# Weight sums made by accumulating loads, one half of x kept on chip, and two more tiles of the pooling gate in the seven-product scheme

## The chip, the cores and the metric

The kernel runs on one core of a Trainium2 chip. The metric is the device time of one execution in microseconds, lower is better; of several executions the median is given. PE is the matrix engine (TensorE), DVE the vector engine, ACT the scalar engine, POOL the GpSimd engine, SP the engine that issues most loads. POOL issues the rest of the transfers, among them all stores of intermediate results.

## The reference

One residual layer over x of 1024 tokens by 1024 channels, float32:

```python
n = rmsnorm(h, norm_mix_pre)
proj = n @ w_in                      # pooling input | q, k, v | xq | three gates of 1024 columns
gates = sigmoid(proj[..., o2:])      # 3 x 1024 channels
y_pool = pool_mixer(p_in, w_pool_mix, pool_scale) @ w_pool_o
y_sb = stick_breaking_attention(q, k, v) @ w_sb_o        # 8 heads, strictly causal
y_x = memory_cross_attention(xq, rmsnorm(mem), w_mem_kv) @ w_x_o
merged = gates[0] * y_pool + gates[1] * y_sb + gates[2] * y_x
h = h + rmsnorm(merged @ w_out, norm_mix_post)
h = h + rmsnorm(swiglu(rmsnorm(h), w_ffn_in) @ w_ffn_out, norm_ffn_post)
```

## The kernel before

Tokens are cut into two halves c = 0, 1 of 512 columns, channels into eight tiles of 128. Each float32 operand is split into a high part (a cast to fp32r on ACT, the first line of `parts` or `split`) and a low part (a subtraction on DVE, the second line), and every product is made as three matmuls (`mm3`: high by high, high by low, low by high).

Projections for a pair of output tiles m, m+1 are a two by two block product, made with seven block products instead of eight (`opening` and `pairs`). Of the weights it needs four quarters b11, b21, b12, b22 (`quarters`, tiles "b", eight slots in all) and three sums of them, t = b12 - b11, then b22 - t, then b21 - t; of the activations it needs A11, A12, A22 and the sums S1 to S4, which are made once before the pairs start and stay in the pools act, a and b1. One block product is 12 matmuls of 512 columns, so a pair is 84. PE's order within a pair is 11, 12 (opening), S1, S2, S4, S3, then the opening of the next pair, then 22. The split weights go through five slots (`wh`, `wl`).

The pairs run for xq, q (two pairs), k (two pairs); then v, in a form of its own with 256 columns; then the pooling gate's tiles 0 to 5 (`PAIRED = 6`, three pairs). Between products, steps of the memory attention and of the pooling mixer are called (`aside`). The remaining gate tiles are made directly, 12 matmuls per unit of (tile, half of the inner sum, half of the tokens): `later` lists 66 such units, and `fill` runs 4 of them before the attention over all tokens ("sticks"), 54 spread over its 32 units by the share of work in each, and 8 after it. Sigmoid, the scan, the mask and the transposes of the sticks run on ACT, DVE, POOL and PE, so the fill units are what PE does meanwhile.

x is loaded once in the beginning (L221, tiles "d") for the pooling input and for the sums of squares, and loaded again in `normed_x` (L256) when the norm is known: half c = 0 around 25 to 33 us into tiles "c" and "d" for A11 and A12, half c = 1 at 55 to 60 us.

Instruction order on each engine is set ahead of the run by a planner that places instructions by priority (roughly the program order) in an estimated timeline; only SP's loads are pinned to the program's order. At run time each engine takes its own list in order and waits on semaphores.

Of the kernel before, what the change touches and what calls it, by code (L numbers as in the profile page):

```python
# [8 lines left out]
F32 = mybir.dt.float32  # L9
F32R = mybir.dt.float32r  # L10
AF = mybir.ActivationFunctionType
ALU = mybir.AluOpType
PSUM = bass.MemoryType.PSUM

P = 128
# [13 lines left out]
LEAD = 8  # L29
HOLD = 3  # L30
EARLY = 3
PAIRED = 6
FILL_FIRST = 4
FILL_LAST = 8
TB = C // P
# [4 lines left out]
def hybrid_block(  # L40
# [47 lines left out]
    def t_act():  # L88
        return act.tile([P, C], F32R, tag="act", name="act")
# [10 lines left out]
    def t_c(dt=F32):  # L100
        return cp.tile([P, C + 16], dt, tag="c", name="c")

    def t_d(dt=F32):
        return dp.tile([P, C + 16], dt, tag="d", name="d")
# [7 lines left out]
    def load(dst, src, queue=nc.sync):  # L112

        if dst.dtype == F32R and queue is not nc.gpsimd:
            dst, src = dst.bitcast(F32), src.bitcast(F32)
        tc.keep_in_program_order(queue.dma_start(dst, src))
# [94 lines left out]
    def pool_step(k):  # L211
        wh, wl = w_units[k]
        for g in range(3):
            for c in range(NC):
                gs = slice(g * P, (g + 1) * P)
                mm3(pp[g][c], wh[:, gs], wl[:, gs], xgh[k][c], xgl[k][c], k == 0, k == KT - 1)

    for k in range(KT):
        for c in range(NC):
            xr = t_d()[:, :C]  # L220
            load(xr, x[k, c])  # L221
            if c == 0:
                w_units[k] = split(w_pool[k], 3 * P)
            nc.scalar.activation(xgh[k][c], xr, AF.Copy, scale=gain(G_PRE, k))
            xgl[k][c] = (t_b1 if k < 4 else t_b2)(F32R)
            nc.vector.scalar_tensor_tensor(
                xgl[k][c], xr, gain(G_PRE, k), xgh[k][c].bitcast(F32), ALU.mult, ALU.subtract
            )
            if k == 0:
                nc.scalar.activation(ssum[c], xr, AF.Square)  # L230
            else:
                sq = t_c()[:, :C]
                nc.scalar.activation(sq, xr, AF.Square)
                nc.vector.tensor_add(ssum[c], ssum[c], sq)
        if k > 3:
            pool_step(k - 4)
# [7 lines left out]

    HK = KT // 2
    A = {n: [None] * HK for n in ("11", "12", "21", "22", "S1", "S2", "S3", "S4")}

# [2 lines left out]
        eng.tensor_sub(lo, src, hi.bitcast(F32))  # L252
        return hi, lo

    def normed_x(k, c, t):
        load(t, x[k, c])  # L256
        nc.vector.scalar_tensor_tensor(t, t, gain(G_PRE, k), rbc[c], ALU.mult, ALU.mult)
        return t

# [16 lines left out]
    units = [split(w_pool_l[half]) for half in range(2)]  # L276
    pc = ps_t()
    rbc = []
    a11 = []
    for c in range(NC):  # L280
        rb = t_r()[:, :C]
        rms_rows(ssum[c], C, pc[:, c * TB : (c + 1) * TB], rb)
        rbc.append(rb)
        pool_step(4 + c)
        if c == 1:
            first_mk = [split(w_mk[0, half]) for half in range(2)]
            first_gate = [t_g(), t_g()]
            for half in range(2):
                load(first_gate[half], w_gate[KT, half])
        else:  # L290
            for q in range(HK):
                a11.append(normed_x(q, 0, t_c()[:, :C]))
                A["11"][q] = parts(a11[q], t_act(), t_act())
    for q in range(4):
        sq = t_c()[:, :C]
        nc.scalar.activation(sq, mr[q], AF.Square)
# [7 lines left out]
    for k in range(6, KT):  # L304
        pool_step(k)
    for q in range(HK):
        u = normed_x(q + HK, 0, t_d()[:, :C])
        A["12"][q] = parts(u, t_act(), t_act())
    raw_d = [
        [dram.tile([P, C], F32, name=f"raw{g}{c}") for c in range(NC)] for g in range(4)  # L310
    ]
# [118 lines left out]
    def quarters(src, m):  # L430

        raw = [[None, None], [None, None]]
        for h, i in ((0, 0), (1, 0), (0, 1), (1, 1)):
            raw[h][i] = t_b2()
            load(raw[h][i], src[m + i, h])
        return raw

    def opening(raw, sink, other=ps_a):
        (b11, b12), (b21, b22) = raw
        X, Y = ps_a(), other()  # L440
        product(X, w_parts(b11), "11", True)
        p1 = copied(X)
        product(Y, w_parts(b21), "12", True)
        nc.vector.tensor_add(p1, Y, p1)
        sink(0, 0, p1)
        return X

    def pairs(jobs, raws=None):

        raws = raws or [jobs[0][0]()]  # L450
        ahead = len(raws)

        opened = [opening(raws[j], jobs[j][1], (ps_a, ps_z)[j]) for j in range(ahead)]
        for j, (_, sink) in enumerate(jobs):
            (b11, b12), (b21, b22) = raws[j]
            if len(raws) == j + 1 < len(jobs):
                raws.append(jobs[j + 1][0]())
            X, Y = opened[j], ps_a()
            t = b11
            nc.vector.tensor_sub(t, b12, t)  # L460
            product(Y, w_parts(t), "S1", True)
            s5 = copied(Y)
            aside()
            nc.vector.tensor_sub(t, b22, t)
            product(X, w_parts(t), "S2")
            s2 = copied(X)
            product(Y, w_parts(b22), "S4")
            nc.vector.tensor_add(s2, Y, s2)
            sink(0, 1, s2)
            aside()  # L470
            nc.vector.tensor_sub(b12, b22, b12)
            product(X, w_parts(b12), "S3")
            nc.vector.tensor_add(s5, X, s5)
            sink(1, 1, s5)
            nc.vector.tensor_sub(b21, b21, t)
            if len(opened) == j + 1 < len(jobs):
                opened.append(opening(raws[j + 1], jobs[j + 1][1]))
            product(X, w_parts(b21), "22")
            sink(1, 0, X)
            aside()  # L480

# [40 lines left out]
    for q in range(HK):  # L522
        room = t_d if q < 3 else t_r
        sums[q], a22[q] = normed_x(q, 1, room()[:, :C]), normed_x(q + HK, 1, room()[:, :C])
        nc.vector.tensor_add(sums[q], sums[q], a22[q])
        A["S1"][q] = parts(sums[q], t_act(), t_act())
    xq_raws = [quarters(w_xq, 0)]
    early(1)
    xq_raws.append(quarters(w_q, 0))
    early(2)  # L530
    for q in range(HK):
        nc.vector.tensor_sub(sums[q], sums[q], a11[q])
        A["S2"][q] = parts(sums[q], t_a(F32R), t_a(F32R))
    for q in range(HK):
        u = t_c()[:, :C]
        nc.vector.tensor_sub(u, A["12"][q][0].bitcast(F32), sums[q])
        nc.vector.tensor_add(u, A["12"][q][1].bitcast(F32), u)
        A["S4"][q] = parts(u, t_a(F32R), t_a(F32R))
    for q in range(HK):
        nc.vector.tensor_sub(sums[q], a22[q], sums[q])  # L540
        A["S3"][q] = parts(sums[q], t_b1(F32R), t_b1(F32R))
    for q in range(HK):
        A["22"][q] = parts(a22[q], t_act(), t_act())
# [221 lines left out]
            split_v(ts[b // 2][:, (b % 2) * W : (b % 2 + 1) * W], 4, t)  # L765
            nc.gpsimd.dma_start(v_d[c * TB + b][i], t)

    def sub2(dst, x_, y_):
        for j in range(2):
            nc.vector.tensor_sub(dst[j], x_[j], y_[j])  # L770

    (b11, b12), (b21, b22) = raw
    X, Y = [ps_a(), ps_a()], [ps_a(), ps_z()]
# [5 lines left out]
        nc.vector.tensor_add(p2[i], X[i], p2[i])  # L779
    to_values(0, 0, p2)  # L780
    aside()
    sub2(b11, b12, b11)
    v_product(Y, two(b11), "S1", True)
    s5 = [copied(t) for t in Y]
    aside()
    sub2(b11, b22, b11)
    v_product(X, two(b11), "S2")
    s2 = [copied(t) for t in X]
    aside()
    v_product(Y, two(b22), "S4")  # L790
    for i in range(2):
        nc.vector.tensor_add(s2[i], Y[i], s2[i])
    to_values(0, 1, s2)
    aside()
    sub2(b12, b22, b12)
    v_product(X, two(b12), "S3")
    for i in range(2):
        nc.vector.tensor_add(s5[i], X[i], s5[i])
    to_values(1, 1, s5)
    aside()  # L800
    sub2(b21, b21, b11)
    v_product(X, two(b21), "22")
    to_values(1, 0, X)

# [596 lines left out]
```

## Time and profile before

| | us |
|---|---|
| median of 3 runs (1493.18 to 1497.05) | 1496.27 |
| the profiled execution's own time | 1493.03 |
| its span in the trace | 1491.3 |
| PE busy | 1446.5 (97%) |
| DVE busy | 1032.1 (69%) |
| ACT busy | 702.0 (47%) |
| POOL busy | 333.6 (22%) |

Read by stages: 0 to 53 us pooling input, to 66 us keys and values of the memory, to 99 us the first direct gate units and the openings of xq and q, to 211 us the pairs of xq, q and k, to 254 us v, to 335 us the three pairs of the pooling gate, to about 630 us the sticks with the fill units, then the merge, the output projection and the feed-forward part. Matmuls overlap, so a PE that is busy throughout a stretch is best measured by the number of matmuls in it.

### The profile page before, as it was taken

What the parts mean: (1) busy time and instruction counts of PE and PEld (TensorE: products, weight loads), DVE (VectorE), ACT (ScalarE), POOL (GpSimd) and SP (SyncE); (2) the same over time, 40 slices, a digit from 0 to 9 for tenths busy, and PEclk for the clock granted to TensorE, in tenths of its full rate; (3) what the DMA queues carried; (4) which work ended last, traced back from release to release, by engine and by line L of the source; (5) the groups of instructions that cost most, each with busy time, mean ns of one, the idle gap of its engine ahead of it and who ended that gap; (6) DMA issues with size and microseconds to landing.
All of it is one profiled execution on the core that took longest, in us unless ns stands there. A gap on an engine that the chain in (4) does not pass through costs nothing.

```text
span 1491.3 us, 21003 instructions
## 1 busy us (share of the span) xinstructions
PE 1446.5 (97%) x6926; PEld 1201.3 (81%) x6926; DVE 1032.1 (69%) x1722; ACT 702.0 (47%) x1399; POOL 333.6 (22%) x612
## 2 busy tenths in 40 slices
PE   9989999889999899999999999999999999999997
PEld 8768889668888788878887777888888887788876
DVE  8797878786876878654515597765566666579476
ACT  8555655444655666521235673233333333444453
POOL 0211121222422432454445310000011111000011
PEclk9989999999999999999999999999999999999999
DMA  8724455565432441585455454444455555664445
GB/s 282 247 74 138 154 180 171 184 211 191 129 103 89 151 126 65 172 265 156 148 163 191 148 183 150 152 128 125 140 195 190 195 191 198 233 191 153 109 129 196
DMA packets 126222, 245.77 MB, mean 165 GB/s; under 512 B 16656, under 2 KB 20256, under 8 KB 126112
## 3 DMA queue, kind: packets, MB, share of 16 engines
q1 hardware_dynamic: 97952, 173.09, 37.3%
q0 software_dynamic: 27584, 70.29, 13.6%
q8 instruction: 54, 0.88, 0.2%
q10 hardware_dynamic: 576, 1.05, 0.2%
q14 instruction: 56, 0.46, 0.1%
HBM read 174.11 MB, written 69.73 MB: 164 GB/s over the span
## 4 chain that ended last, share of the span: by engine, by line
PE 84%; DVE 6%; issue 4%; DMA 3%; ACT 2%; POOL 1%; SPq 0%; POOLq 0%; DVEq 0%; ACTq 0%
PE pa L170 17%; PE pa L172 17%; PE pa L171 17%; PE pz L172 5%; PE pz L171 5%; PE pz L170 5%; PE pt L172 3%; PE pt L170 3%; PE pt L171 3%; PE pt L893 2%; PE pv L908 1%; PE pv L905 1%; PE pv L171 1%; PE pv L170 1%; PE pv L172 1%
## 5 line engine op out<-in xcount | busy, mean ns | idle before, releaser
L170 PE MATMUL pa<-act,wh 128*128 128x512 f32 (+1 forms) x584 | 230.6, 395 | 10.8 <-ACT wh L164 3.5
L172 PE MATMUL pa<-act,wl 128*128 128x512 f32 (+1 forms) x584 | 229.8, 396 | 3.9 <-DVE wl L252 3.8
L171 PE MATMUL pa<-act,wh 128*128 128x512 f32 (+1 forms) x584 | 230.0, 394 | 0.0
L251 ACT CAST wh<-b 128x512 fp32r<-128x512 f32 x152 | 93.5, 621 | 146.4 <-PE pa L171 86.3
L170 PEld LDWEIGHTS pa<-act,wh 128*128 128x128 f32 x584 | 111.3, 191 | 34.8 <-issue 4.1
L172 PEld LDWEIGHTS pa<-act,wl 128*128 128x128 f32 x584 | 111.4, 191 | 27.0 <-DVE wl L252 5.2
L171 PEld LDWEIGHTS pa<-act,wh 128*128 128x128 f32 x584 | 111.1, 190 | 20.9
L252 DVE TENSOR_TENSOR wl<-b,wh 128x512 fp32r<-128x512 f32 x152 | 103.2, 685 | 30.7 <-ACT wh L251 26.0
L164 ACT CAST wh<-ws 128x512 fp32r<-128x512 f32 (+1 forms) x119 | 72.7, 612 | 104.4 <-PE pa L171 34.2
L251 ACT CAST wh<-ws 128x512 fp32r<-128x512 f32 x80 | 49.9, 625 | 106.6 <-DVE ws L1165 42.1
L165 POOL TENSOR_TENSOR wl<-ws,wh 128x512 fp32r<-128x512 f32 x52 | 69.3, 1340 | 72.4 <-ACT wh L164 70.1
L251 ACT CAST d<-b 128x512 fp32r<-128x512 f32 x66 | 40.7, 620 | 90.6 <-PE pt L171 45.8
L252 DVE TENSOR_TENSOR d<-b,d 128x512 fp32r<-128x512 f32 x66 | 45.3, 689 | 51.0 <-ACT d L251 50.9
L165 DVE TENSOR_TENSOR wl<-ws,wh 128x512 fp32r<-128x512 f32 (+1 forms) x67 | 44.7, 672 | 51.7 <-ACT wh L164 31.0
L170 PE MATMUL pa<-a,wh 128*128 128x512 f32 x192 | 75.9, 398 | 2.6 <-ACT wh L251 1.2
L171 PE MATMUL pa<-b,wh 128*128 128x512 f32 x192 | 75.0, 392 | 0.0
L172 PE MATMUL pa<-a,wl 128*128 128x512 f32 x192 | 74.6, 392 | 0.0
L176 DVE TENSOR_TENSOR d<-pt,d 128x512 fp32r<-128x512 f32 (+1 forms) x96 | 60.6, 637 | 16.9 <-ACT d L175 16.1
L1131 POOL DMA_DIRECT2D ff<-c x44 | 23.8, 542 | 214.9 <-DVE c L1186 123.6
L175 ACT CAST d<-pt 128x512 fp32r<-128x512 f32 (+1 forms) x96 | 53.0, 559 | 36.4 <-PE pt L893 25.5
L252 DVE TENSOR_TENSOR wl<-ws,wh 128x512 fp32r<-128x512 f32 x80 | 54.9, 688 | 17.8 <-ACT wh L251 15.4
L181 POOL TENSOR_TENSOR rc<-rv,mhalf 128x1 f32<-128x1 f32 (+2 forms) x15 | 14.5, 969 | 229.8 <-DVE rv L1294 198.3
(422 smaller groups left out, 4026.7 us busy)
## 6 DMA issues: line engine op xcount, KB each, us to landing
b<-in_w_ffn_in_dram SPq DMA_DIRECT2D x88, 256.0 KB, 2.8
d<-gt SPq DMA_DIRECT2D x48, 256.0 KB, 2.8
ws<-in_w_ffn_in_dram SPq DMA_DIRECT2D x44, 256.0 KB, 2.7
ff<-c POOLq DMA_DIRECT2D x44, 256.0 KB, 3.2
b<-ffS SPq DMA_DIRECT2D x44, 256.0 KB, 2.6
ws<-in_w_gate_dram SPq DMA_DIRECT2D x40, 256.0 KB, 3.4
gt<-g POOLq DMA_DIRECT2D x39, 256.0 KB, 2.8
b<-ff SPq DMA_DIRECT2D x33, 256.0 KB, 3.6
```

What stands on the lines that cost most here:

```text
L164: nc.scalar.copy(wh[:, :n], ws[:, :n])
L165: lo.tensor_sub(wl[:, :n], ws[:, :n], wh[:, :n].bitcast(F32))
L170: nc.tensor.matmul(ps, lh, rh, start=first, stop=False, skip_group_check=onto)
L171: nc.tensor.matmul(ps, lh, rl, start=False, stop=False, skip_group_check=onto)
L172: nc.tensor.matmul(ps, ll, rh, start=False, stop=last, skip_group_check=onto)
L175: nc.scalar.copy(hi, ps)
L176: nc.vector.tensor_sub(lo, ps, hi.bitcast(F32))
L251: nc.scalar.copy(hi, src)
L252: eng.tensor_sub(lo, src, hi.bitcast(F32))
L893: nc.tensor.transpose(ptr[:, col + n * P : col + (n + 1) * P], att[i, j // 4][:, (j % 4) * P : (j % 4 + 1) * P], ident,)
L905: nc.tensor.matmul(po[:, :wd], vs, al[:, at : at + wd], start=j2 == t2 and n == 0, stop=False)
L1131: nc.gpsimd.dma_start(ff_d[n][k], t)
```

## The change

Three edits. (1) In `quarters`, `opening` and `pairs` the DVE subtractions that made the weight sums are gone. The signs of S1, S2, S3 and S4 are turned so that each sum is an addition, and the addition is done by a transfer that POOL issues (`onto`): it reads a quarter of the weights again from DRAM and adds it to what lies in the tile. The tile of b11 goes through b11, b11 + b21 ..., each step after the parts of the last were taken. The results of S4 and S3 are now subtracted from (`less`, a three-operand instruction on DVE). For v the sums stay on DVE, with other signs. (2) Half c = 0 of x is loaded into eight tiles of the pool act (32 slots) and stays there; it is scaled in place and read for A11, A12 and the sums S2 and S4, where S4 takes one instruction per tile instead of two. (3) `PAIRED` is 8: the pooling gate's tiles 6 and 7 become a fourth pair, and `later` shrinks from 66 units to 58.

```diff
-PAIRED = 6
+PAIRED = 8
...
+    xs = []
     for k in range(KT):
         for c in range(NC):
-            xr = t_d()[:, :C]
+            if c == 0:
+                xr = act.tile([P, C], F32, tag="act", name="act")
+                xs.append(xr)
+            else:
+                xr = t_d()[:, :C]
             load(xr, x[k, c])
...
-    def normed_x(k, c, t):
-        load(t, x[k, c])
+    def normed_x(k, c, t, kept=False):
+        if not kept:
+            load(t, x[k, c])
...
-                a11.append(normed_x(q, 0, t_c()[:, :C]))
-                A["11"][q] = parts(a11[q], t_act(), t_act())
+                A["11"][q] = parts(normed_x(q, 0, xs[q], True), t_act(), t_act())
...
-        u = normed_x(q + HK, 0, t_d()[:, :C])
-        A["12"][q] = parts(u, t_act(), t_act())
+        A["12"][q] = parts(normed_x(q + HK, 0, xs[q + HK], True), t_act(), t_act())
...
-        return raw
+        onto(raw[0][1], src[m + 1, 1])
+        return raw, src[m : m + 2]
+
+    def onto(t, src):
+        nc.gpsimd.dma_start(t, src, accum_op=ALU.add)
+
+    def less(t, ps):
+        nc.vector.scalar_tensor_tensor(t, ps, -1.0, t, ALU.mult, ALU.subtract)
 
     def opening(raw, sink, other=ps_a):
-        (b11, b12), (b21, b22) = raw
+        ((b11, _), (b21, _)), src = raw
         X, Y = ps_a(), other()
         product(X, w_parts(b11), "11", True)
+        onto(b11, src[1, 0])
         p1 = copied(X)
...
-            (b11, b12), (b21, b22) = raws[j]
+            ((t, t3), (_, b22)), src = raws[j]
...
-            t = b11
-            nc.vector.tensor_sub(t, b12, t)
             product(Y, w_parts(t), "S1", True)
+            onto(t, src[1, 1])
             s5 = copied(Y)
             aside()
-            nc.vector.tensor_sub(t, b22, t)
             product(X, w_parts(t), "S2")
+            onto(t, src[0, 1])
             s2 = copied(X)
             product(Y, w_parts(b22), "S4")
-            nc.vector.tensor_add(s2, Y, s2)
+            less(s2, Y)
             sink(0, 1, s2)
             aside()
-            nc.vector.tensor_sub(b12, b22, b12)
-            product(X, w_parts(b12), "S3")
-            nc.vector.tensor_add(s5, X, s5)
+            product(X, w_parts(t3), "S3")
+            less(s5, X)
             sink(1, 1, s5)
-            nc.vector.tensor_sub(b21, b21, t)
             if len(opened) == j + 1 < len(jobs):
                 opened.append(opening(raws[j + 1], jobs[j + 1][1]))
-            product(X, w_parts(b21), "22")
+            product(X, w_parts(t), "22")
...
-        nc.vector.tensor_add(sums[q], sums[q], a22[q])
+        nc.vector.tensor_sub(sums[q], a22[q], sums[q])
...
-        nc.vector.tensor_sub(sums[q], sums[q], a11[q])
+        nc.vector.scalar_tensor_tensor(
+            sums[q], sums[q], -1.0, xs[q], ALU.mult, ALU.subtract
+        )
...
-        u = t_c()[:, :C]
-        nc.vector.tensor_sub(u, A["12"][q][0].bitcast(F32), sums[q])
-        nc.vector.tensor_add(u, A["12"][q][1].bitcast(F32), u)
+        u = xs[q + HK]
+        nc.vector.scalar_tensor_tensor(u, u, -1.0, sums[q], ALU.mult, ALU.subtract)
...
-        nc.vector.tensor_sub(sums[q], a22[q], sums[q])
+        nc.vector.scalar_tensor_tensor(
+            sums[q], sums[q], -1.0, a22[q], ALU.mult, ALU.subtract
+        )
```

## Rows read from the trace of the kernel before

**Rows 1.** The page's first part: busy us, share of the span, instructions.

```profile
PE 1446.5 (97%) x6926; PEld 1201.3 (81%) x6926; DVE 1032.1 (69%) x1722; ACT 702.0 (47%) x1399; POOL 333.6 (22%) x612
```

**Rows 2.** What PE waited for, 66 to 335 us: total us, times, longest.

```profile
PE pa L170 <- ACT wh L164: 3.5, 1, 3.5
PE pa L170 <- DVE d L359: 3.5, 1, 3.5
PE pa L172 <- DVE wl L252: 2.2, 1, 2.2
```

**Rows 3.** Stretches: length, then busy us (instructions) of PE, PEld, DVE, ACT, POOL; clock; DMA.

```profile
98.40:113.00 14.60, 10.56 (x29) 7.32 (x28) 12.84 (x22) 5.42 (x11) 2.14 (x4) 0.65 0.41 126
281.00:335.00 54.00, 50.02 (x214) 39.39 (x212) 46.72 (x84) 27.35 (x47) 12.10 (x23) 1.00 0.59 186
350.00:630.00 280.00, 273.77 (x1521) 233.67 (x1520) 221.47 (x340) 166.51 (x370) 96.90 (x255) 1.00 0.38 121
370.00:430.00 60.00, 58.06 (x329) 49.63 (x328) 54.41 (x85) 39.12 (x88) 20.87 (x64) 1.00 0.38 117
490.00:510.00 20.00, 16.54 (x82) 12.62 (x83) 18.86 (x27) 14.30 (x32) 13.19 (x20) 1.00 0.43 148
510.00:610.00 100.00, 100.00 (x565) 86.11 (x564) 83.17 (x127) 61.37 (x134) 33.61 (x95) 1.00 0.32 100
1000.00:1050.00 50.00, 50.00 (x222) 41.42 (x221) 26.16 (x40) 19.23 (x33) 2.71 (x5) 1.00 0.44 136
```

**Rows 4.** PE in order of time, 98 to 112 us: start, us, instruction, idle before.

```profile
99.35 0.47 PE L170 MATMUL pa<-act,wh 128*128 128x512 f32 x1 [0.59 <-DVE c L444]
...
102.26 0.79 PE L172 MATMUL pa<-act,wl 128*128 128x512 f32 x1 [2.22 <-DVE wl L252]
...
106.27 0.63 PE L172 MATMUL pa<-act,wl 128*128 128x512 f32 x1
108.13 0.80 PE L170 MATMUL pa<-a,wh 128*128 128x512 f32 x1 [1.24 <-ACT wh L251]
```

**Rows 5.** DVE's groups, 76 to 109 us: busy us, mean ns, idle before.

```profile
L537 DVE TENSOR_TENSOR c<-act,c 128x512 f32<-128x512 f32 x4 | 2.7, 684 | 0.0
L460 DVE TENSOR_TENSOR b<-b,b 128x512 f32<-128x512 f32 x2 | 1.4, 683 | 0.0
L471 DVE TENSOR_TENSOR b<-b,b 128x512 f32<-128x512 f32 x2 | 1.4, 683 | 0.0
```

**Rows 6.** DVE in order of time, 98 to 109.5 us: start, us, instruction.

```profile
100.32 0.68 DVE L471 TENSOR_TENSOR b<-b,b 128x512 f32<-128x512 f32 x1
...
101.53 0.68 DVE L252 TENSOR_TENSOR wl<-b,wh 128x512 fp32r<-128x512 f32 x1
...
106.34 0.68 DVE L464 TENSOR_TENSOR b<-b,b 128x512 f32<-128x512 f32 x1
...
108.14 0.68 DVE L475 TENSOR_TENSOR b<-b,b 128x512 f32<-128x512 f32 x1
108.75 1.28 DVE L252 TENSOR_TENSOR wl<-b,wh 128x512 fp32r<-128x512 f32 x2
```

**Rows 7.** DVE, ACT and PE in order of time, in the first pair of k.

```profile
162.72 0.68 DVE L252 TENSOR_TENSOR wl<-b,wh 128x512 fp32r<-128x512 f32 x1
...
164.42 0.62 ACT L251 CAST wh<-b 128x512 fp32r<-128x512 f32 x1 [0.96 <-DVE b L464]
...
169.22 0.39 PE L170 MATMUL pa<-a,wh 128*128 128x512 f32 x1
```

**Rows 8.** POOL's group of k's stores: busy us, mean ns, idle before.

```profile
L558 POOL DMA_DIRECT2D k<-d x16 | 8.5, 533 | 26.3 <-ACT d L251 22.9 <-DVE d L252 2.6 <-DVE st L592 0.5
```

**Rows 9.** Transfers, 255 to 335 us: issuing queue, count, KB each, median us to landing.

```profile
v<-d POOLq DMA_DIRECT2D x12, 256.0 KB, 4.7
...
gt<-c POOLq DMA_DIRECT2D x9, 256.0 KB, 2.3
```

**Rows 10.** DVE by form: a three-operand instruction with a PSUM source.

```profile
L686 DVE SCALAR_TENSOR_TENSOR d<-pv,g_sb,d 128x512 fp32r<-128x512 f32 x8 | 6.0, 748 | 4.8 <-ACT d L685 4.8
```

More of the change, by code (lines that the diff above doesn't have):

```diff
@@ L278, in hybrid_block @@
     rbc = []
-    a11 = []
     for c in range(NC):
@@ L766, in to_values, with add2 @@
             nc.gpsimd.dma_start(v_d[c * TB + b][i], t)
-    def sub2(dst, x_, y_):
+    def add2(dst, x_):
         for j in range(2):
-            nc.vector.tensor_sub(dst[j], x_[j], y_[j])
+            nc.vector.tensor_add(dst[j], dst[j], x_[j])
     (b11, b12), (b21, b22) = raw
@@ L781, in hybrid_block @@
     aside()
-    sub2(b11, b12, b11)
+    add2(b11, b12)
     v_product(Y, two(b11), "S1", True)
@@ L785, in hybrid_block @@
     aside()
-    sub2(b11, b22, b11)
+    add2(b11, b22)
     v_product(X, two(b11), "S2")
@@ L791, in hybrid_block @@
     for i in range(2):
-        nc.vector.tensor_add(s2[i], Y[i], s2[i])
+        less(s2[i], Y[i])
     to_values(0, 1, s2)
     aside()
-    sub2(b12, b22, b12)
+    add2(b12, b22)
     v_product(X, two(b12), "S3")
     for i in range(2):
-        nc.vector.tensor_add(s5[i], X[i], s5[i])
+        less(s5[i], X[i])
     to_values(1, 1, s5)
     aside()
-    sub2(b21, b21, b11)
+    add2(b21, b11)
     v_product(X, two(b21), "22")
```

## The prediction, made before the changed kernel was run

> **What bounds the kernel now.** I read the page's busy line first: PE works 97% of the span, every other engine 69% or less [rows 1]. So only two things can shorten the run: fewer matmuls, or less of PE's idle time and low clock. Next the windows: in a full stretch PE gets through 222 matmuls of 512 columns in 50 us [rows 3], that is 50 / 222 = 0.225 us each, 2.70 us for a block product of 12 and 18.9 us for a pair of 84. Then the waits of PE over the stages that the change touches: the three longest are a gate weight at 69 us (3.5), v's last evictions at 267 us (3.5) and a low part of weights at 100 us (2.2) [rows 2]. The reader is to see that the edits reach only the third. The timeline of PE shows what it costs: the product S1 of xq begins at 99.35, stops for 2.22 at its third matmul, and S2 of xq begins only at 108.13 [rows 4]. Meanwhile the granted clock falls: it averages 0.65 over 98.4 to 113, against 1.00 in the full stretches, so part of it ran at 1.2 instead of 2.4 GHz [rows 3]. The instructions from 102.26 to 106.27 are 10 and the next 8 begin at a spacing of about 0.43 us, 0.20 more than at full clock.
>
> **Why there.** DVE is the cause: from 76 to 109 us its groups have no idle time before them [rows 5], and it starts one instruction about every 0.60 us (108.14 to 108.75 [rows 6]). It works through the sums of activations, which come first in the program, and through the weights' sums; the low part of S1 of xq is made at 101.53 and that of S2 at 108.75 [rows 6].
>
> **The change part by part.**
>
> *Products.* Tiles 6 and 7 of the pooling gate cost 2 x 2 x 2 units of 12 matmuls, 96; as a pair they cost 84. 12 x 0.225 = 2.7 us less on PE, which is the bound, so it counts in full: -2.7.
>
> *DVE's queue at 76 to 109 us.* Removed: the second instruction of S4 (L537, 4), the weight subtractions L460 and L471 (2 each) [rows 5] and one each of L464 and L475 [rows 6]: 10 x 0.60 = 6.0 us. Added: 12 of the activation sums become three-operand instructions, 748 ns by the nearest row [rows 10] against 684 [rows 5], 12 x 0.06 = 0.7. Ahead of S1's low part stand seven of the ten, so it starts at about 101.5 - 4.2 + 0.6 = 97.9 and PE runs S1 straight on, done near 101.5. S2 of xq was allowed by DVE at 108.75; now near 108.75 - 6.0 + 0.7 = 103.4. But its weights now come by a transfer that can start only when S1's low part is read: 98.6 + D + a cast of 0.62, where D is issue and landing of an accumulating load. PE would start S2 near 103.7 instead of 108.13, 4.4 less, and its first 8 matmuls would run at full clock, 8 x 0.20 = 1.6 less: together -6.0. Bounds: -7.6 if no wait is left at all (0.59 + 2.22 + 1.24 of idle [rows 4] and 18 x 0.20 = 3.6 of clock), and 0 or above if D is long. A gap of 2.2 before S2 remains possible, and the clock fell behind a gap of 2.22 before [rows 4], which would take back some 2 us, so I take -5.0.
>
> *D.* No accumulating load is in the trace. POOL's issue takes 0.53 us [rows 8]; plain transfers of the same 256 KB from POOL's queue land 2.3 us after issue, 4.7 where the queue is full of v's small pieces [rows 9]. An accumulating load also has to read the tile that it adds to. Lower end 0.5 + 2.3 = 2.8, upper end 0.5 + 2 x 4.7 = 9.9; I take 0.5 + 4.0 = 4.5, nearer the row under load. The Trainium skill ("DMA: Bandwidth & Descriptors", Anatomy of one DMA) gives such a POOL-issued transfer about 2 us plus its bytes over 436 GB/s, an estimate of 2.6 us; the median rows here lie on both sides of it. By it S2 of xq would wait for DVE alone, and the sum would change by 0.3 us.
>
> *The other pairs.* Nine pairs carry four accumulating loads each. Where does the chain through t have room? In the first pair of k, S1's low part starts at 162.72 and ends at 163.40; S2's cast is at 164.42 and PE uses it at 169.22 [rows 7]. The room is 169.22 - 163.40 - 0.62 = 5.2 us, and D = 4.5 fits. In the other links (11 to S1, S2 to 22) two or more products of 2.7 us lie between, and the sum in b12's tile is made ahead. So nothing is added at this D; at 9.9, 4.7 us per pair. What goes from DVE is four instructions of 0.68 a pair. In the gate pairs DVE is busy 46.7 of 54.0 us and PE idles 4.0 [rows 3]; taking 2.5 pairs x 2.7 = 6.8 us off DVE should about halve that: -2.0 (bounds 0 and -4). POOL gains 36 issues of 0.53, 19 us over stages of 250 us, on an engine that is 22% busy [rows 1]; it takes its queue in order, though, so a sum may stand behind a store that waits for an eviction, and the store behind a sum whose readers are late. The Trainium skill (the same page, Two DMAs through the same engine are not ordered) has it that a transfer which depends on another must be held at the issuing engine until the first has landed. So POOL waits for the load of b12 before each first sum, with the sink's stores behind it. No row shows such a wait; I price it inside D's bounds.
>
> *The fourth pair.* 84 matmuls are in the products' term; its own idle time by the other gate pairs is 4.0 / 2.5 = 1.6 us, half of it with DVE relieved: +0.8.
>
> *Fewer fill units.* Inside the sticks 54 units become 46, so PE has 8 x 2.70 = 21.6 us less to do in the 280 us that hold nearly all of it; that is the other side of the pair's 18.9. DVE there is busy 221.5 of 280, 79%; after, four splits fewer, (221.5 - 2.7) / (280 - 21.6) = 85%. Where DVE is at 83% (510 to 610) PE idles nowhere; where it is at 91 to 94% (370 to 430 and 490 to 510, 73.3 of 80 us) PE idles 1.94 + 3.46 = 5.4 of 80, or 6.8% [rows 3]. 85% is nearest the first: (84.7 - 83.2) / (91.6 - 83.2) x 6.8% x 258 = 3.0: +3.0; bounds 0 and +11 (the whole step from 79% to 85% on that slope).
>
> *x kept on chip.* Eight loads fewer; they landed before 53 us, where PE runs without a pause, so nothing (bounds 0 and -1). S1's parts now take slots that the memory's parts leave at 66 us; they are needed at 99. The gate weight that PE waits 3.5 us for at 69 us [rows 2] is behind the loads for half c = 1, which stay. Two sums join that burst: up to +2, not counted.
>
> Sum: -2.7 - 5.0 - 2.0 + 0.8 + 3.0 = -5.9 us. Against the profiled execution, 1493.0, that is 1487.1. It lies 3.2 below the median of the runs shown, so I put the same difference on the median: 1496.3 - 5.9 = 1490.4.
>
> **The rivals.**
> *Slow sums (slower than before).* D decides, from about 5.2 us on, where S2 becomes late in each pair. At D = 7.5: 2.3 us in each of 8 pairs = 18, and at xq the whole -5.0 goes. 1490.4 + 18 + 5 = 1513. For it: another stream to read, POOL's order, DMA shares of 0.41 to 0.59 in these stages [rows 3]. Against it: every plain row from this queue is under 5. Chance 0.21.
> *Starved sticks (no change).* PE follows DVE once there are fewer fill units: +11 instead of +3.0, 1498. For it 370 to 430, against it 510 to 610 [rows 3]. Chance 0.15.
> *The queue at 98 us is only exchanged (no change).* S2 of xq waits for its transfer instead of DVE; the -5.0 is gone, 1495. For it: 103.7 and 103.4 stand close, so each us of D counts. Chance 0.14.
> *The change doesn't do what it says:* the planner lays out all engines by estimated times, and may put S4 before S2 or let a late sum block ACT's queue; inside the ranges above.
>
> **How the numbers follow.** The forecast has a chance of 0.50, its own range 1483 to 1493. Within 0.3% (4.5 us) of before, about what runs of this kernel can tell from no change, lie the second and third rival: 0.29. Slower 0.21. Faster 0.50. The range goes from 1481 (no wait left at 98 us, no starved sticks) to 1505, which takes in slow sums up to D of about 6.5.
>
> **What would show it.** Right: S2 of xq starts near 104 instead of 108.1, clock above 0.9 over 98 to 113; accumulating loads landing in 4 us or less; PE's idle share in the sticks under 4%; DVE's busy time about 19 us less (36 instructions of 0.68 gone, 30 longer by 0.06, the new pair 4 more). Wrong: casts of weights that wait for a POOL transfer with PE idle behind them in the pairs of k and the gate; landings above 5 us; idle PE before transposes and values in the sticks above 10 us.

## The result, and the profile after

The changed kernel takes 1509.05 us (median of 4 runs, 1505.63 to 1511.21) against 1494.72 of the kernel before in the same comparison: a ratio of 1.0099, interval 1.0079 to 1.0118. It is slower by 14.3 us, where 5.9 us less had been forecast, and lies 4 us above the upper end of the range.

The section on the change names the first sum wrongly: the tile of b11 goes b11, then b11 + b12, then + b22, then + b21, for src[1, 0] is the quarter b12.

The busy line of the kernel after, beside [rows 1], then its line for the transfers that POOL issues (packets, MB, and the time of these packets as a share of 16 engines' span):

```profile
PE 1451.4 (96%) x6914; PEld 1205.0 (80%) x6914; DVE 1014.1 (67%) x1692; ACT 704.8 (47%) x1405; POOL 361.2 (24%) x648
...
q0 software_dynamic: 32768, 79.73, 17.4%
```

The same line of the kernel before:

```profile
q0 software_dynamic: 27584, 70.29, 13.6%
```

PE has 12 matmuls fewer and DVE is busy 18.0 us less, as the change intends. PE is idle 13 us longer, though (1509.2 - 1451.4 = 57.8 against 1491.3 - 1446.5 = 44.8), and its busy time is 4.9 us longer in spite of the missing matmuls. POOL's queue grew by 9.44 MB, 36 x 256 KB, but its share of the engines by (17.4% x 1509.2 - 13.6% x 1491.3) / 36 = 1.66 us of all 16 engines for each added transfer.

Where it is lost is seen in the windows. Columns as in [rows 3]. The kernel after: the stretch of S2 of xq, one in the gate pairs, the sticks, and all from the first pair to the end of the gate pairs:

```profile
98.40:113.00 14.60, 11.48 (x37) 8.49 (x37) 6.78 (x12) 4.82 (x9) 3.41 (x5) 0.77 0.71 178
281.00:335.00 54.00, 53.71 (x230) 43.82 (x231) 42.34 (x78) 26.83 (x46) 20.06 (x31) 0.98 0.83 216
390.00:655.00 265.00, 252.67 (x1408) 215.22 (x1407) 211.38 (x330) 158.47 (x355) 93.49 (x250) 0.99 0.36 112
...
100.00:365.00 265.00, 241.04 (x1246) 204.32 (x1247) 173.86 (x359) 130.22 (x277) 77.66 (x126) 0.95 0.70 188
```

The kernel before, 100 to 365 us:

```profile
100.00:365.00 265.00, 251.04 (x1313) 212.13 (x1313) 202.19 (x404) 138.25 (x292) 55.71 (x108) 0.97 0.57 177
```

DVE, which stood in front of PE before, does 28 us less there, and PE gets through 67 matmuls fewer (of several sizes, so the count is rough). The DMA engines' share rose from 0.57 to 0.70; in the gate pairs it is 0.83 where it was 0.59 [rows 3]. Marks in PE's timeline of several profiled executions tell the same by stages (the last column is the last matmul into pt that reads weights; the kernel before has three gate pairs, the others four, and a pair is 18.9 us). The execution of the kernel after that was profiled is its slowest, 1511.2 us, so its marks lie some us later than the medians do:

| us | S2 of xq starts | v starts | v ends | last S3 of the gate ends | into pt |
|---|---|---|---|---|---|
| before | 108.1 | 211.1 | 257.6 | 330.0 | 738.6 |
| after | 102.2 | 216.0 | 262.4 | 365.9 | 757.6 |
| after, sums on DVE | 102.9 | 208.6 | 255.5 | 350.8 | 740.1 |
| after, no sums | 93.4 | 199.0 | 246.3 | 338.6 | 730.9 |
| sums on DVE, loads into dead tiles | 104.7 | 214.3 | 261.7 | 362.5 | 753.5 |

So 5.9 us are won up to S2 of xq, 10.8 lost from there to v, nothing in v (which has no such load), and some 12 more in the gate pairs than the pair that was added. Behind 760 us the kernels run alike.

What PE waits for after, 66 to 365 us:

```profile
PE pa L170 <- ACT wh L257: 10.1, 4, 3.9
...
PE pz L603 <- DVE st L605: 2.9, 1, 2.9
```

The second of these can be followed back. All engines of the kernel after in order of time, first pair of k:

```profile
159.76 0.68 DVE L258 TENSOR_TENSOR wl<-b,wh 128x512 fp32r<-128x512 f32 x1
...
161.01 0.89 POOL L445 DMA_DIRECT2D b<-in_w_k_dram  x1 [5.39 <-DVE st L605]
...
164.94 1.66 ACT L257 CAST wh<-b 128x512 fp32r<-128x512 f32 x3 [3.58 <-DMA b<-in_w_k_dram]
165.59 1.29 DVE L258 TENSOR_TENSOR wl<-b,wh 128x512 fp32r<-128x512 f32 x2 [3.75 <-ACT wh L257]
...
166.92 0.76 DVE L605 TENSOR_REDUCE st<-pz 128x1 f32<-128x256 f32 x2
...
167.73 0.58 PE L603 MATMUL pz<-c,r 128*128 128x256 f32 x1 [2.90 <-DVE st L605]
```

S1's low part ends at 160.44, POOL issues the sum (the releaser named is the DVE instruction behind that low part), ACT casts S2 at 164.94: D is 4.5 us, the forecast's value. PE does not run out of S2, but DVE waits 3.75 us in its own queue for that cast, the reduction for the memory attention stands behind it, and PE waits 2.90 us for the reduction. The room of 5.2 us in the forecast had been read up to PE's use of S2 alone.

POOL's groups after, 60 to 365 us (busy us, mean ns of one, idle before), beside [rows 8]:

```profile
L572 POOL DMA_DIRECT2D k<-d x16 | 9.2, 649 | 27.2 <-ACT d L257 22.9 <-DVE d L258 3.7 <-issue 0.6
...
L445 POOL DMA_DIRECT2D b<-in_w_k_dram x8 | 7.1, 934 | 20.0 <-DVE wl L258 8.1 <-DMA b<-in_w_k_dram 6.5 <-DVE st L605 5.4
```

Transfers after, 66 to 355 us (median us to landing):

```profile
k<-d POOLq DMA_DIRECT2D x16, 256.0 KB, 4.1
...
b<-in_w_gate_dram POOLq DMA_DIRECT2D x16, 256.0 KB, 5.7
...
r<-xq SPq DMA_DIRECT2D x16, 128.0 KB, 3.8
b<-in_w_k_dram SPq DMA_DIRECT2D x8, 256.0 KB, 6.6
b<-in_w_k_dram POOLq DMA_DIRECT2D x8, 256.0 KB, 4.2
```

And before, same stretch:

```profile
k<-d POOLq DMA_DIRECT2D x16, 256.0 KB, 3.5
...
r<-xq SPq DMA_DIRECT2D x16, 128.0 KB, 2.9
b<-in_w_k_dram SPq DMA_DIRECT2D x8, 256.0 KB, 5.4
```

An accumulating load's issue keeps POOL 0.93 us, not 0.53, and it lands in 4.2 to 5.7 us. Its neighbours in these rows, from either queue, land later too. The Trainium skill ("DMA: Bandwidth & Descriptors", Issuing engines are not separate DMA queues) says that transfers run on the same 16 engines whichever engine issued them. The rows for k fit that, since SP's loads went from 5.4 to 6.6 us; not every group does (v's stores went from 4.6 to 3.8 us).

### The profile page after: what moved, and what is told of

Its sections match the earlier page's. It is cut to its first block, busy times and chain, and to the rows that moved or that the text cites. A ratio compares the mean times of both kernels' runs of the same rounds, so it can differ in the third digit from the quotient of the medians.

```text
span 1509.2 us, 21025 instructions
## 1 busy us (share of the span) xinstructions
PE 1451.4 (96%) x6914; PEld 1205.0 (80%) x6914; DVE 1014.1 (67%) x1692; ACT 704.8 (47%) x1405; POOL 361.2 (24%) x648
## 3 DMA queue, kind: packets, MB, share of 16 engines
q0 software_dynamic: 32768, 79.73, 17.4%
HBM read 181.45 MB, written 69.73 MB: 166 GB/s over the span
## 4 chain that ended last, share of the span: by engine, by line
PE 74%; issue 8%; DMA 7%; DVE 6%; POOL 3%; ACT 2%; SPq 0%; POOLq 0%; DVEq 0%; ACTq 0%
PE pa L170 14%; PE pa L172 13%; PE pa L171 13%; PE pz L172 5%; PE pz L170 5%; PE pz L171 5%; PE pt L170 3%; PE pt L171 3%; PE pt L172 3%; DMA b<-in_w_gate_dram 2%; PE pt L907 1%; DMA ws<-in_w_gate_dram 1%; PE pv L919 1%; PE pv L922 1%; PE pv L170 1%
## 5 line engine op out<-in xcount | busy, mean ns | idle before, releaser
L170 PE MATMUL pa<-act,wh 128*128 128x512 f32 (+1 forms) x568 | 224.0, 394 | 8.1 <-DVE d L363 2.9
L171 PE MATMUL pa<-act,wh 128*128 128x512 f32 (+1 forms) x568 | 222.5, 392 | 0.0
L172 PE MATMUL pa<-act,wl 128*128 128x512 f32 (+1 forms) x568 | 220.8, 392 | 1.3 <-DVE wl L258 1.2
L257 ACT CAST wh<-b 128x512 fp32r<-128x512 f32 x159 | 96.8, 620 | 158.8 <-PE pa L171 68.8
L258 DVE TENSOR_TENSOR wl<-b,wh 128x512 fp32r<-128x512 f32 x159 | 107.7, 686 | 56.5 <-ACT wh L257 48.0
L170 PEld LDWEIGHTS pa<-act,wh 128*128 128x128 f32 x568 | 107.7, 190 | 32.2 <-ACT wh L257 4.2
L172 PEld LDWEIGHTS pa<-act,wl 128*128 128x128 f32 x568 | 107.5, 189 | 23.4 <-DVE wl L258 2.1
L171 PEld LDWEIGHTS pa<-act,wh 128*128 128x128 f32 x568 | 107.7, 190 | 20.5 <-issue 0.2
L257 ACT CAST wh<-ws 128x512 fp32r<-128x512 f32 x76 | 47.4, 624 | 109.2 <-DVE ws L1179 39.8
L170 PE MATMUL pa<-a,wh 128*128 128x512 f32 x200 | 81.7, 412 | 11.1 <-ACT wh L257 9.3
L257 ACT CAST d<-b 128x512 fp32r<-128x512 f32 x66 | 40.8, 621 | 91.9 <-PE pt L171 47.0
L172 PE MATMUL pa<-a,wl 128*128 128x512 f32 x200 | 79.7, 402 | 0.0
L171 PE MATMUL pa<-a,wh 128*128 128x512 f32 x160 | 65.0, 406 | 0.0
L888 DVE TENSOR_TENSOR_SCAN r<-a,zero 128x512 f32<-128x512 f32 (+1 forms) x64 | 53.5, 843 | 16.1 <-POOL a L876 15.5
```

What stands on the lines that cost most here:

```text
L170: nc.tensor.matmul(ps, lh, rh, start=first, stop=False, skip_group_check=onto)
L171: nc.tensor.matmul(ps, lh, rl, start=False, stop=False, skip_group_check=onto)
L172: nc.tensor.matmul(ps, ll, rh, start=False, stop=last, skip_group_check=onto)
L257: nc.scalar.copy(hi, src)
L888: nc.vector.tensor_tensor_scan(ex[:, lo + 1 : C + 1], rest[:, lo:], zero.broadcast_to([P, C - lo]), start, ALU.mult, ALU.add,)
```

## The experiments

The two theories that last longest stood at first. **A**, the chain: casts of weights wait in ACT's and DVE's in-order queues for an accumulating load, as at 164.94. **C**, the transfers: an accumulating load takes so much of the 16 engines that loads and stores around it come late, whoever waits for it. A third, **B**, came up on the way: POOL's in-order queue, in which a load waits until DVE has made a low part and stores stand behind it. (In the first four expectations B is another rival, that the fourth pair starves the sticks.) Each run is told as its median and its ratio to the kernel before, run beside it, with the 95% interval.

**Parts of the change.** All sums on DVE (e1), six tiles paired (e2), the sum loads alone (e3), x kept alone (e5).

```diff
# e1, on the changed kernel (all four sums alike)
-            onto(t, src[1, 1])
+            nc.vector.tensor_add(t, t, b22)
             product(X, w_parts(t), "S2")
# e2
-PAIRED = 8
+PAIRED = 6
# e3: e2 with x loaded again in normed_x;  e5: e1 with PAIRED = 6
```

e1: 

> The changed kernel with all weight sums back on DVE (additions, new signs), x kept, eight paired tiles. Theory A (a cast of a summed tile waits in ACT's in-order queue for POOL's transfer, and what stands behind it on ACT and DVE is late): the pairs of q and k lose their 10.8 us and the gate pairs some 9 us, so about 1489 us, and no cast waits for a transfer from POOL. Rival B (the fourth pair starves the sticks, the sums are harmless): about 1505. Rival C (DMA traffic and slower stores, not the waits): about 1489 as well; later runs tell A from C.

e2: 

> The changed kernel with six paired tiles of the pooling gate as before, sums by transfers and x kept stay. Theory A: the sums' losses in q and k (10.8 us) and in three gate pairs (about 6 us) stay, the fourth pair's and the sticks' (about 10 us) go: about 1500. Rival B: about 1489, below the kernel before. Rival C: about 1500.

e3: 

> The kernel before with the weight sums made by accumulating loads and nothing else (x loaded twice, six paired tiles, S4 in two instructions). Theory A: slower than before, about 1503 (10.8 in q and k, about 6 in the gate pairs, less up to 6 us gained at 98 us where DVE is full). Rival B: 1489 to 1495. Rival C: about 1503.

e5: 

> The kernel before with x's first half kept and the S4 sums in one instruction, weight sums on DVE, six paired tiles. Theory A and B: four of DVE's instructions fewer ahead of 101 us, so S1 and S2 of xq 2 to 3 us earlier: 1490 to 1493. Rival D (keeping x costs by slots of act): 1495 or more.

Measured: e1 1492.89 us, 0.9991 (0.9979 to 1.0003). e2 1501.72, 1.0053 (1.0036 to 1.0070). e3 1501.24, 1.0055 (1.0034 to 1.0076). e5 1493.58, 0.9997 (0.9986 to 1.0009). Sticks starved by the fourth pair would have left e1 at 1505, so that rival fell. The whole loss goes with the sum loads: they cost 1509.1 - 1492.9 = 16 us with eight tiles paired and 1501.7 - 1493.6 = 8 us with six. Keeping x (with S4 in one instruction) is worth nothing, and the pair of tiles 6 and 7 nothing that can be told apart (e1 against e5). Why the price per pair rises with the fourth pair (8 us for 8 pairs, 16 for 9) was not settled.

**What the sums cost.** No sums (e4): the four accumulations are left out, so the products use other weights. Plain loads in their place (e6): same tiles, same waits, the data replace instead of adding.

```diff
# e4
-            onto(t, src[1, 1])
# e6
-        nc.gpsimd.dma_start(t, src, accum_op=ALU.add)
+        nc.gpsimd.dma_start(t, src)
```

e4: 

> The changed kernel with the four accumulating loads left out and nothing in their place: the products S1, S2, S3 and 22 take the quarter as it was loaded, so the weight sums are missing from the computation. Theory A (casts wait for transfers): back to about 1490, like the sums on DVE (1492.9) and at most 3 us lower, for DVE has slack there. Rival C (traffic): the same, 1488 to 1492.

e6: 

> The changed kernel with plain loads from POOL's queue in place of the accumulating ones, same tiles, same waits, so the tile holds the last quarter instead of the sum. Theory A: any transfer on the chain costs nearly the same, 1502 to 1509, issue 0.5 instead of 0.9 us and landing about a us sooner. Rival E (accumulation itself is what is slow): below 1497.

Measured: e4 1484.39, 0.9919 (0.9897 to 0.9942); e6 1495.32, 0.9999 (0.9983 to 1.0015). Without sums and loads the kernel is 10.5 us faster than the kernel before and 8.5 faster than e1, which differs from e4 by DVE's sums; both theories had expected less. The accumulating loads cost 24.7 us against none, and 13.7 of these go when the same loads only write: e6 lies where rival E, the accumulation itself, had put it, and not where theory A had. The line of POOL's transfers, e6:

```profile
q0 software_dynamic: 30464, 79.73, 15.6%
```

The same bytes at a smaller share of the engines: (15.6% x 1497.2 - 13.6% x 1483.6) / 36 = 0.88 us each (e4's line has 13.6% too), about half of an accumulating load's 1.66.

**The chain or the transfers.** e8 has DVE's sums and issues the four accumulating loads into tiles that nobody reads any more, so no cast waits for one. e9 shortens the chain instead: the sums of S1 and S2 are built ahead in tiles of their own, for two more plain loads and one more accumulating load a pair.

```diff
# e8, on e1
+            onto(b22, src[1, 0])      # behind the last reader of b22
             product(X, w_parts(b12), "S3")
+            onto(b12, src[1, 1])
...
             nc.vector.tensor_add(b21, b21, t)
+            onto(t, src[0, 1])
...
             product(X, w_parts(b21), "22")
+            onto(b21, src[0, 0])
# e9, on the changed kernel
+        u = [t_c()[:, :C], t_c()[:, :C]]
+        for i in range(2):
+            load(u[i], src[m, 0])
+            onto(u[i], src[m + 1, 0])
+        onto(u[1], src[m + 1, 1])
```

e8: 

> Weight sums on DVE (the variant that took 1492.9), and four accumulating loads a pair beside them, each into a tile whose last reader is done, so that no cast waits for one: POOL's issues and the bytes of the changed kernel without its waits. Theory A: 1493 to 1497. Rival C (traffic, slower stores, POOL's time): 1503 to 1509.

e9: 

> The changed kernel with the sums of S1 and S2 built in tiles of their own, straight after the loads (two more loads by SP and one more accumulating load a pair), so that no cast of theirs waits for the readers of the product before; only the sum for 22 follows S2's parts. Theory A: most of the loss goes, 1493 to 1500, though the traffic is higher. Rival C: 1509 or more.

Measured: e8 1509.34, 1.0092 (1.0074 to 1.0109); e9 1513.13, 1.0118 (1.0101 to 1.0135). Theory A fell as the whole cause: with no cast waiting for the data, the loads cost 16.4 us over e1, as much as the changed kernel loses against e1. But it keeps a share. Where DVE makes no sums, the loads cost 24.7 us, 8.3 more than into dead tiles. And e9, with 9 more accumulating and 18 more plain loads, is only 4.1 us slower than the changed kernel; at the prices of e8 and of e10 below (16.4 / 36 and 6.6 / 36 us a load) these would add 7.4, an estimate. In the changed kernel PE waits twice in the gate pairs for S2's cast, which waits for its load, 3.9 us at 272 and 3.0 at 348; e8 has no such wait there. The second of them:

```profile
347.70 1.14 ACT L257 CAST wh<-b 128x512 fp32r<-128x512 f32 x2 [6.50 <-DMA b<-in_w_gate_dram]
348.37 0.75 PE L170 MATMUL pa<-a,wh 128*128 128x512 f32 x1 [2.98 <-ACT wh L257]
```

So the 8.3 us may be the chain's; that is not shown, since no run takes the chain out without adding traffic.

e1's queue line and window:

```profile
q0 software_dynamic: 27584, 70.29, 13.4%
...
100.00:365.00 265.00, 251.23 (x1321) 213.74 (x1322) 199.27 (x400) 136.76 (x287) 54.59 (x104) 0.98 0.57 175
```

e8's, with POOL's group of these loads in the gate pairs and POOL's longest wait, 60 to 365 us:

```profile
q0 software_dynamic: 32768, 79.73, 17.4%
...
100.00:365.00 265.00, 244.45 (x1275) 206.74 (x1274) 196.94 (x398) 133.13 (x281) 83.26 (x132) 0.95 0.76 198
...
L444 POOL DMA_DIRECT2D b<-in_w_gate_dram x16 | 15.2, 948 | 20.4 <-DVE wl L258 19.5 <-DVE d L704 0.8
...
POOL b L444 <- DVE wl L258: 32.8, 16, 5.0
```

46 matmuls fewer in the window at 0.225 us [rows 3] are 10.4 us; the marks above say 11.7 up to the last S3. What reaches PE can be followed at its two longest waits in e8 that are longer than in e1.

The first is in SP's queue. No cast waits for the dead loads, but SP's next loads into their slots do, and SP's loads go out in order too. The loads that bring xq back for the memory attention stand behind four that wait for slots of xq's weights. They are issued at 116.31 in e8 and at 106.24 in e1, and PE waits 3.3 us for them instead of 1.3. SP in e8:

```profile
110.71 5.50 SPq L116 DMA_DIRECT2D b<-in_w_q_dram  x4
116.31 1.29 SPq L116 DMA_DIRECT2D r<-xq  x2
```

The second is PE's longest wait in e8, early in the gate pairs. ACT makes a result of the pooling mixer, POOL stores it (`ph`), and a later cast needs a tile whose store has to land first. e1, then e8:

```profile
258.64 0.69 ACT L699 ACTIVATE d<-pv,g_sb 128x512 fp32r<-128x512 f32 x1
...
259.62 0.53 POOL L704 DMA_DIRECT2D ph<-d  x1 [4.44 <-ACT d L362]
...
262.80 0.50 PE L170 MATMUL pv<-d,wh 128*128 128x512 f32 x1 [1.00 <-ACT d L257]
```

```profile
264.78 0.69 ACT L703 ACTIVATE d<-pv,g_sb 128x512 fp32r<-128x512 f32 x1
...
267.12 1.47 POOL L708 DMA_DIRECT2D ph<-d  x2
...
273.08 0.62 ACT L257 CAST d<-c 128x512 fp32r<-128x512 f32 x1 [4.70 <-DMA ph<-d]
...
273.75 0.79 PE L170 MATMUL pv<-d,wh 128*128 128x512 f32 x1 [5.79 <-ACT d L257]
```

In e1 the store is issued 0.3 us after its data and no cast waits for it. In e8 it is issued 1.6 us after its data, behind two of the dead loads, and holds the cast until 6.0 us after its issue, so PE waits 5.8 us instead of 1.0. The larger part is the landing, but POOL's queue has a share, and theory B stays open: the last line shown for POOL in e8 has it waiting 32.8 us for DVE's low parts.

**Transfers or POOL's queue.** e10 is e8 with plain loads, e11 is e8 with accumulating loads of half the columns. Neither changes what POOL's loads wait for.

```diff
# e10
-        nc.gpsimd.dma_start(t, src, accum_op=ALU.add)
+        nc.gpsimd.dma_start(t, src)
# e11
+        nc.gpsimd.dma_start(t[:, : C // 2], src[:, : C // 2], accum_op=ALU.add)
```

e10: 

> The kernel with DVE's sums and four transfers a pair into tiles that nobody reads any more (1.0092 of the kernel before), with plain loads in place of the accumulating ones: the same number of issues on POOL, the same waits there, the same stores behind them; the four loads' data are not used. Theory C (the accumulating transfer itself: its 16-engine time of 1.66 us against 0.88, and its issue of 0.94 us against 0.53): more than half of the 16.4 us goes, 1496 to 1501 us. Rival B (POOL's queue is in order, so stores stand behind a load that waits for DVE's cast, whatever the load does): nothing goes, 1505 to 1510 us.

e11: 

> The same kernel with accumulating loads of half the columns (256 of 512) into the tiles that nobody reads: same issues and waits, half the bytes, the same number of packets or half. Theory C in its form 'bytes and packets that read, add and write': 1499 to 1503 us, about half of the loss. If the issue of an accumulating load on POOL or its fixed part is what costs, the time stays at 1506 to 1510 us. Rival B expects 1505 to 1510 us too.

Measured: e10 1499.52, 1.0038 (1.0019 to 1.0056); e11 1497.89, 1.0022 (1.0008 to 1.0037). e10's lines, then e11's:

```profile
q0 software_dynamic: 30464, 79.73, 15.5%
...
L444 POOL DMA_DIRECT2D b<-in_w_gate_dram x16 | 8.7, 544 | 20.4 <-DVE wl L258 20.3
...
POOL b L444 <- DVE wl L258: 35.7, 17, 5.0
```

```profile
q0 software_dynamic: 32768, 75.01, 15.5%
...
L444 POOL DMA_DIRECT2D b<-in_w_gate_dram x16 | 15.2, 953 | 17.0 <-DVE wl L258 16.0 <-DVE d L704 0.8
...
POOL b L444 <- DVE wl L258: 31.6, 14, 5.0
```

e10 falls into theory C's range; e11 is below all of its ranges. These two settle most of it. e11 keeps e8's issue time on POOL (953 and 948 ns), its packets (32768) and its waits (31.6 and 32.8 us), and loses 5.0 us over e1 instead of 16.4. e10 keeps the bytes at a shorter issue, and loses 6.6. What the two have in common is the share of the 16 engines, 15.5%, where e8 has 17.4% and e1 13.4%: above e1's 200.0 us that is 0.89 and 0.90 us a load against 1.73. So neither the bytes, nor the waits and packets, nor the time that POOL's issues take is the whole cost; the kernel's time goes with the engines' time. Half of it costs 5 to 7 us, all of it 16. With intervals of 2 to 3 us either side that may or may not be in proportion, and how e11's 5.0 us divide between POOL's longer issues and its bytes is not shown.

**The rest of theory B.** e14 and e15 issue e8's and e10's loads later in the program, behind the pair's stores. e18, e17 and e16 tie them to the end of a product by a one-column copy into their tile: copies alone, with plain loads, with accumulating loads.

```diff
# e14 (e15 plain)
             sink(1, 0, X)
+            onto(t, src[0, 1])
+            onto(b21, src[0, 0])
# e16 (e17 plain, e18 without the load)
+        nc.vector.tensor_copy(t[:, :1], ps[:, :1])
         nc.gpsimd.dma_start(t, src, accum_op=ALU.add)
```

e14: 

> The kernel with DVE's sums and four accumulating loads a pair into tiles that nobody reads any more (1.0092), with each load issued a product or more later, after the pair's stores, when the casts that read the tile are long done: the same transfers, and POOL no longer waits for a cast with stores behind it. Theory C (the engines' time that the accumulating transfers take): 1504 to 1510 us. Rival B' (that time hurts by way of POOL's queue, where a load that waits for a cast holds up the stores): 1496 to 1501 us.

e15: 

> The same with plain loads, whose data are not used. With waits they cost 5 to 7 us over the kernel with DVE's sums (1499.5 against 1492.9). If the bytes are what is left of the cost: 1496 to 1500 us. If the waits in POOL's queue are: 1492 to 1495 us.

e18: 

> The kernel with DVE's sums, x kept and eight tiles paired, plus four copies of one column a pair from a product's result into tiles that nobody reads any more, and no load: the base for the next two. Both theories: 1491 to 1496 us.

e17: 

> The same with a plain load from POOL's queue behind each copy, into the same tile (its data are not used). It waits for a product's end, as the stores beside it do, no longer for a cast of weights ahead of them. Theory C (bytes on the 16 engines): 3 to 7 us over the base. Rival B' (POOL's queue held by a load that waits for a cast): 0 to 2 us over the base.

e16: 

> The same with accumulating loads behind the copies. Theory C: 11 to 16 us over the base, as where they waited for casts. Rival B': 4 to 8 us.

Measured: e14 1505.89, 1.0070 (1.0045 to 1.0095); e15 1499.63, 1.0035 (1.0021 to 1.0050); e18 1498.73, 1.0045 (1.0029 to 1.0060); e17 1505.74, 1.0079 (1.0050 to 1.0108); e16 1517.75, 1.0166 (1.0141 to 1.0191). Neither set did what it was meant to. The planner put the loads of e14 into the very places of e8 on POOL, so e14 and e15 repeat e8 and e10, and agree with them within 3.5 us. The copies cost 6 us by themselves, against the expectation, and they lengthened POOL's waits for the loads instead of ending them. POOL's longest wait is 32.3 us in e14; in e17 and in e16 it is:

```profile
POOL b L445 <- DVE b L444: 69.0, 21, 8.5
```

```profile
POOL b L445 <- DVE b L444: 60.9, 19, 9.0
```

They still say something. e14 and e15 lie where theory C and the bytes had been put, e17 at the upper end of theory C's range and e16 3 us above it. Plain loads cost 6.6 us over their base at 36 us of POOL's waiting (e10) and 7.0 at 69 (e17), so POOL's waiting is not visibly what they cost; accumulating loads cost 16.4 (e8) and 19.0 (e16). The surplus of adding over writing at the same places is 9.8, 6.3 and 12.0 us (e8 and e10, e14 and e15, e16 and e17). How a plain load's 5 to 7 us divide between its bytes and POOL's waits stays open: no kernel without these waits was tried.

**Other places for the sums.** e12 makes all four sums on POOL, e13 only those of S3 and 22.

```diff
# e13, on e1 (e12: all four)
-            nc.vector.tensor_add(b12, b12, b22)
+            nc.gpsimd.tensor_add(b12, b12, b22)
```

e12: 

> The changed kernel with its four sums a pair made as additions on POOL, in place of accumulating loads; x kept, eight tiles paired. No sum stands in DVE's queue and no byte is moved twice. If the sums were dear by the transfers, this stands between the kernel with DVE's sums (1492.9) and the one without sums (1484.4): 1485 to 1492 us. Rival: a POOL addition of 512 columns (1.34 us in the row of the pooling steps) stands on the chain of S1 and S2 and ahead of stores in POOL's queue, and slows DVE beside it: 1495 to 1503 us.

e13: 

> The same with only the sums of S3 and of the last product on POOL, where a product or more lies between sum and use; S1's and S2's stay on DVE. If POOL's additions cost nothing when nothing waits for them: about half of what DVE's sums cost against none (8.5 us) comes back, 1487 to 1491 us. If they slow DVE or the stores behind them: 1493 to 1498 us.

Measured: e12 1498.39, 1.0026 (1.0011 to 1.0041); e13 1491.82, 0.9986 (0.9970 to 1.0001). POOL's additions are no free replacement: e12 lies where its rival had been put, e13 between its two ranges. e12's groups of POOL and DVE, 60 to 365 us:

```profile
L471 POOL TENSOR_TENSOR b<-b,b 128x512 f32<-128x512 f32 x9 | 25.0, 2782 | 13.0 <-DVE wl L258 6.3 <-DVE c L671 3.9 <-DVE fix L687 2.5
L475 POOL TENSOR_TENSOR b<-b,b 128x512 f32<-128x512 f32 x9 | 13.3, 1475 | 12.7 <-DVE wl L258 9.4 <-ACT d L257 3.2
```

```profile
L258 DVE TENSOR_TENSOR wl<-b,wh 128x512 fp32r<-128x512 f32 x77 | 60.9, 798 | 17.5 <-ACT wh L257 17.1
```

The first sum of a pair takes 2.78 us there, and DVE's low parts 798 ns instead of 0.68 us [rows 6]. e13 and e1 leave nothing out and beat the changed kernel by 17 and 16 us; neither can be told from the kernel before.

## Why the prediction was wrong

- *What bounds the kernel:* right. PE is at 96%, and the loss is idle time and low clock of PE before 760 us.
- *Products, fourth pair, fill units (-2.7 + 0.8 + 3.0 = +1.1):* right within what the runs tell with DVE's sums: e1 lies 0.7 us under e5. With the accumulating loads the same three terms come to +7 (after against e2). In the sticks PE idles 12.3 of 265 us, 4.7%, where the forecast allowed 4% and it was 6.2 of 280 [rows 3]. By the marks, the stretch behind the gate pairs became 19.3 us shorter in e1 and 16.9 after, though 21.6 us of matmuls left it: +2.3 and +4.7 in place of +3.0.
- *DVE's queue at 98 us (-5.0):* right at its place, by the path that the forecast named. S2 of xq begins at 102.2 instead of 108.1 [rows 4] and waits for its transfer. Two terms of that path were off against each other: S1's low part ended at 96.0 (95.33 + 0.69), not 98.6, and D was 5.5 us, not 4.5. The parts of the change don't add up here: S2 begins at 103.9 with x kept and no loads (e5), at 102.2 with the loads alone (e3), and neither kernel is faster for it. It was wrong that the clock would hold. Behind the gap of 2.43 us the matmuls are 0.43 us apart, as they were before, up to 109.4, and the window has 0.77, not 0.9. The cast and PE, after:

```profile
101.53 1.66 ACT L257 CAST wh<-b 128x512 fp32r<-128x512 f32 x3 [3.65 <-DMA b<-in_w_xq_dram]
102.20 0.50 PE L170 MATMUL pa<-a,wh 128*128 128x512 f32 x1 [2.43 <-ACT wh L257]
...
104.32 0.63 PE L171 MATMUL pa<-a,wh 128*128 128x512 f32 x1
104.74 0.63 PE L172 MATMUL pa<-a,wl 128*128 128x512 f32 x1
...
109.72 0.40 PE L171 MATMUL pa<-a,wh 128*128 128x512 f32 x1
```

- *D (4.5):* right where it was worked out, in the first pair of k. In the gate pairs the landing alone takes 5.7 us, and in the last of them D was 8.4 us, from the end of S1's low part at 339.27 to S2's cast at 347.70. The Trainium skill's estimate of 2.6 us ("DMA: Bandwidth & Descriptors", Anatomy of one DMA), set beside it in the forecast, is below every median landing of such a load after (4.2 to 5.7 us).
- *The other pairs (-2.0, "nothing is added at this D"):* **this step failed.** It priced a sum by one delay, from S1's low part to PE's use of S2. It counted 36 POOL issues at 0.53 us (they take 0.93) on an engine with time to spare, left the waits in POOL's queue inside D's bounds, and put no term at all for the engines' time, though the forecast had in hand that the load "also has to read the tile that it adds to" and that the DMA shares there were 0.41 to 0.59. e8 shows the cost with no cast waiting: 16.4 us; e10 and e11, that it halves or better with the engines' time. The delay that it did price was not nothing either: the room of 5.2 us was read in a pair of k, and in the gate pairs, where the loads land in 5.7 us, PE waits 3.9 and 3.0 us for S2's cast. The relief of DVE was priced too low, if anything (8.5 us, e4 against e1); it could not stand against 24.7.
- *x kept (0):* right, e5 0.9997. *DVE's busy time (-19; the terms named for it give -20):* -18.0. The three-operand instructions of the activation sums take 684 to 687 ns, as the plain ones do, and not 748.
- *The rivals:* "slow sums" came nearest, 1513 at D = 7.5. Its sign was right, but that its number is near is luck: the loads landed in 4.2 to 5.7 us by the medians. Its mechanism, S2 late in each pair, is there in places (wh L257, 10.1 us of PE's waits), but not in each pair, and e8 loses 16.4 us without it. The rival that was missing is the one that a wider look at [rows 9] offers: the transfers beside it, not the one that is waited for.

## What to carry to other kernels

An addition that a transfer makes is not free because no engine shows it: price it by the time that it takes from the 16 DMA engines, beside their share in that stage, and by the loads and stores that will land later. If a doubt is left whether the wait for the data or the traffic costs, keep the traffic and let nobody read it: that run tells whether the loss needs the wait. Waits in the issuing queues, and for the slots that such transfers hold, stay in it and want a run of their own. A gain at one place (DVE's queue at 98 us) is only a gain if the stages behind it hold it.

## What the runs showed of the hardware that was not expected

- An accumulating load of 256 KB took 1.66 to 1.73 us of all 16 DMA engines, a plain one 0.88 to 0.89; one of 128 KB, accumulating, 0.90. HBM traffic doesn't show it: from e1 to e8 it grew from 172.01 to 181.45 MB read, the loads' bytes once, and stayed at 69.73 MB written.
- Its issue on POOL took 0.89 to 0.96 us in these runs (group means, but for the four loads of xq), the same at both sizes (948 ns for 256 KB, 953 for 128 KB) against 0.54 for a plain one, and k's plain stores, which stand between such loads in the queue, were issued in 649 ns instead of 533 [rows 8].
- An addition on POOL of 512 columns with two operands in SBUF took 1.4 to 2.8 us (e12), and DVE's subtractions in the same stretch 798 ns instead of 686 (e1).
